# Reordering three stage borders of a hybrid mLSTM / gating / macaron block on one core

## The chip, the cores and the metric

The kernel runs on one core of a Trainium2 chip. The metric is the device time of one execution in microseconds (us). TensorE is called PE, VectorE DVE, ScalarE ACT, GpSimd POOL and SyncE SP; POOL and SP mostly start transfers here. PEld is the weight load of TensorE.

## The reference

One layer of a streaming encoder on x of 1024 tokens by 1024 features, in float32, with RMS norms ahead of every part:

```
x += 0.5 * SwiGLU_1(rmsnorm(x) * g1)            # d_ff = 2816
xn = rmsnorm(x) * gm;  P = xn @ w_mix_in
h_m = mlstm(P), 4 heads of 256;  h_s = spatial gating(P)
x += (sigmoid(g_m) * h_m + sigmoid(g_s) * h_s) @ w_mix_out
x += 0.5 * SwiGLU_2(rmsnorm(x) * g2)
out = rmsnorm(x) * final_g
```

## The kernel before

Tokens are held as two halves of 512 (h, or t, = 0 and 1); features lie on the 128 partitions, in eight tiles d = 0 to 7. A float32 operand is split into a rounded high part (ACT cast) and a remainder (DVE subtraction), and each product is three matmuls, high by high, high by low and low by high. One call of `prod` is 12 matmuls of 128x512.

Each SwiGLU input projection is done as a 2x2 block product with seven instead of eight block products. For that, `operands(i, get)` forms sums and differences of the two token halves (tiles "t1" to "t4" and "22"), for i = 0 to 3. While these do not exist yet, PE can only run products with half 0: "11" (features 0 to 3) and "21" (features 4 to 7) of a d_ff tile f. They are done ahead for the first `EARLY` = 9 tiles by `first_product(f)`: "11" into a PSUM bank, an ACT copy of the bank, "21" added into the same bank, an ACT Silu of it. Both results go to DRAM (`eb`) and come back when `group(f)` needs them. `group(f)` is the rest of a tile's work and needs all operands.

**FFN1's opening.** `scales(0)` sums the squares of the tokens (ACT for two token tiles, DVE `bn_stats` for two), forms 1/rms `r` and puts it on four diagonal matrices `dg`. `scaled(0, d)` then transposes and scales at once: a matmul of the token tile with `dg`. ACT and DVE split the result into xn, POOL rebuilds the sum and writes it to DRAM (`xs_`). Then come `first_product(0)`, `scales(1)` for half 1, and four rounds of two `first_product` calls, two `residual(d)` (plain transposes of both halves into `xd[2]`, the residual stream in DRAM) and `operands(i, get)`, where `get` takes half 0 from DRAM and half 1 from `scaled(1, d)` by way of ACT.

**FFN1 to mix.** `Stats` adds squares as the last down projection ends; `bcast` turns them into a scale tile: four small matmuls (L220), a chain of small DVE steps with one ACT square root, four DVE diagonals (L234), one matmul with ones (L237), an ACT copy (L239). `hook1` does this for half 1 at the very end of FFN1, although half 1's normed tiles are only made in the mix, after head 0.

**Mix to FFN2.** `mix_out(1, prev)` ends the mix with its output projection (L157 into `po`) and its own `bcast`; FFN2's first products come after it in the program.

Programs are handed to a scheduler that fixes each engine's order in advance: program order gives the priority, and an instruction that it expects to be ready may go ahead of an earlier one that it expects to wait. On the chip each engine then runs its list in that order. `t512` tiles come from a ring of four in FFN1 and FFN2; raw weights from a ring of three (`rawp`); operands of `operands` from a ring of six (`c512`); `bigp` holds 16 tiles for tokens, xn and operands.

Of the kernel before, what the change touches and what calls it, by code (L numbers as in the profile page):

```python
# [13 lines left out]
P = 128  # L14
S = 1024
D = 1024
NH = 512
# [1 line left out]
DFF = 2816  # L19
NF = DFF // P  # L20
BLOCKS = [(0, 3), (3, 3), (6, 3), (9, 3), (12, 3), (15, 3), (18, 4)]
EARLY = 9
SPAD = 40
MPAD = 24
HEADS = 4
# [8 lines left out]
def block_body(ctx, tc, x, ffn1_norm_g, ffn1_w_in, ffn1_w_out, mix_norm_g, w_mix_in, mlstm_conv_w,  # L34
# [228 lines left out]
    class Ffn:  # L263
# [35 lines left out]
            V.tensor_tensor(out=s, in0=a, in1=b, op=op)  # L299
            return s  # L300

        def first_product(self, f):
            r1, r2 = self.raw(f, 0, False), self.raw(f, 1, False)
            w1, w2 = self.unit(r1[:, :, 0, :]), self.unit(r2[:, :, 0, :])
            a = bank("mm")
            self.prod(a, w1, "11", True, False)
            e = self.hp.tile([P, 2, NH], F32, tag="h", name="early")
            A.copy(out=e[:, 0, :], in_=a)  # L308
            G.dma_start(out=self.eb[f][0], in_=e[:, 0, :])
            self.prod(a, w2, "21", False, True)  # L310
            A.activation(out=e[:, 1, :], in_=a, func=AF.Silu)
            G.dma_start(out=self.eb[f][1], in_=e[:, 1, :])

        def group(self, f):
            r1, r2 = self.raw(f, 0, True), self.raw(f, 1, True)
# [149 lines left out]
    def mix(mx, xnm):  # L465
# [122 lines left out]
        def sgu_v(xn):  # L588
            gz = [bigp.tile([P, D], F32, tag="big", name="gz") for _ in range(4)]
            stt = ss.tile([P, 4, 4, 6], F32, tag="stt", name="stt", bufs=1)  # L590
            gT = ss.tile([P, NC, 8], F32, tag="gT", name="gT")
            for c in range(4):
                if c == 0:
                    b = token_pair_wide(wmi, CZV, (CI, 8), xn)
                else:
                    b = token_pair(wmi, CZV + c * 2 * P, xn)
                for t in range(4):
                    if c == 0:
                        V.tensor_tensor(out=gT[:, t, :], in0=b[t][:, 2 * P:2 * P + 8], in1=bif, op=ALU.add)
                        src = b[t][:, 0:2 * P]  # L600
                    else:
                        src = b[t // 2][:, (t % 2) * 2 * P:(t % 2 + 1) * 2 * P]
                    dst = gz[t][:, c * 2 * P:(c + 1) * 2 * P]
                    A.activation(out=dst, in_=src, func=AF.Gelu)  # L604
                    V.bn_stats(out=stt[:, t, c, :], in_=dst)
                if c == 0:
                    gt = gates(gT)
            mv = ss.tile([P, 4, 2], F32, tag="mv", name="mv")
            for t in range(4):
                V.bn_aggr(out=mv[:, t, :], in_=stt[:, t].rearrange("p c s -> p (c s)"))  # L610
            r = rsqrt(mv[:, :, 1], 4, LN_EPS)
            for t in range(4):
                V.tensor_scalar(out=gz[t], in0=gz[t], scalar1=mv[:, t, 0:1], scalar2=r[:, t:t + 1], op0=ALU.subtract,
                                op1=ALU.mult)
            return gz, gt
# [159 lines left out]
        def mix_out(half, Ms):  # L775
            mh = []
            for ct in range(KT):
                mt = bigp.tile([P, 2, NH], F32R, tag="big", name="mh")
                split(Ms[ct], mt)
                mh.append(mt)  # L780
            st = Stats()
            for d in range(0, KT, 2):
                b = feature_pair(w_mix_out[0], d * P, mh, "po")
                for j in range(2):
                    xr = xrp.tile([P, NH], F32, tag="xr", name="xr")
                    nc.sync.dma_start(out=xr, in_=xd[0][half][d + j])
                    V.tensor_tensor(out=xr, in0=b[j], in1=xr, op=ALU.add)
                    nc.sync.dma_start(out=xd[1][half][d + j], in_=xr)
                    st.add(xr)
            return st.bcast()  # L790

        def reload(dram):
            def ld(d):
# [8 lines left out]
        for half in range(2):  # L802
            xn = xnm[half]
            if half == 0:
                setup()
                gz, gt = sgu_v(xn)
            cur = qkv(0, xn)
            if half == 1:
                bcs.append(mix_out(0, prev))
                gz, gt = sgu_v(xn)  # L810
            Ms = sgu_mix(gz)
            for h in range(HEADS):
                num = mlstm(h, half, *cur, gt)
                Gt = fillers(h, xn, Ms)
                merge(h, num, Gt, Ms)
                if h + 1 < HEADS:
                    cur = qkv(h + 1, xn)
                if h == 0:
                    if half == 0:
                        xnm[1] = normed(reload(xd[0][1]), "gm", xnm[1])  # L820
                    else:
                        xn2[0] = normed(reload(xd[1][0]), "g2", bcs[0], keep=xs_[1])
            prev = Ms
        bcs.append(mix_out(1, prev))
        return xn2[0], bcs

    with f1:
        ffn1 = Ffn(f1, "1", ffn1_w_in[0], ffn1_w_out[0])
        st2 = [Stats(), Stats()]
        dgs = []  # L830
        xns = []
        xnm = [None, None]

        def scales(h):
            dg = sp.tile([P, NH], F32, tag="bc", name="dg", bufs=2)
            ssq = sp.tile([P, 4, 2], F32, tag="ssq", name="ssq", bufs=2)
            stt = sp.tile([P, 2, 8, 6], F32, tag="sst", name="sst", bufs=1)
            for i in range(4):
                for t in range(2):
                    junk = t512()  # L840
                    A.activation(out=junk[:, 0:2 * P], in_=tok[h][i][:, t], func=AF.Square,
                                 accum_out=ssq[:, i:i + 1, t])
                    for j in range(2):
                        V.bn_stats(out=stt[:, t, 2 * i + j, :], in_=tok[h][i][:, t + 2, j, :])
# [14 lines left out]
            for t in range(4):  # L859
                V.tensor_scalar(out=dg[:, t * P:(t + 1) * P], in0=ident, scalar1=r[:, t:t + 1], scalar2=None,  # L860
                                op0=ALU.mult)
            dgs.append(dg)

        def scaled(h, d):
            ps = bank("mm")
            for t in range(4):
                PE.matmul(out=ps[:, t * P:(t + 1) * P], lhsT=tok[h][d % 4][:, t, d // 4, :],
                          rhs=dgs[h][:, t * P:(t + 1) * P], start=(t == 0), stop=(t == 3), skip_group_check=True)
            return ps

        def residual(d):
            xt = ffn1.hp.tile([P, 2, NH], F32, tag="h", name="xres")
            for h in range(2):
                ps = psm()
                for t in range(4):
                    PE.transpose(out=ps[:, t * P:(t + 1) * P], in_=tok[h][d % 4][:, t, d // 4, :], identity=ident)
                V.tensor_copy(out=xt[:, h, :], in_=ps)
                G.dma_start(out=xd[2][h][d], in_=xt[:, h, :])

        def get(j, i, t):  # L880
            b = ffn1.c512()
            if t == 0:
                G.dma_start(out=b, in_=xs_[0][4 * j + i])
            else:
                A.activation(out=b, in_=scaled(t, 4 * j + i), func=AF.Copy, scale=pc("g1", 4 * j + i))
            return b

        scales(0)
        for d in range(KT):
            ps = scaled(0, d)  # L890
            xt = bigp.tile([P, 2, NH], F32R, tag="big", name="xn")
            A.activation(out=xt[:, 0, :], in_=ps, func=AF.Copy, scale=pc("g1", d))
            V.scalar_tensor_tensor(out=xt[:, 1, :], in0=ps, scalar=pc("g1", d), in1=xt[:, 0, :].bitcast(F32),
                                   op0=ALU.mult, op1=ALU.subtract)
            xk = t512()
            G.tensor_tensor(out=xk, in0=xt[:, 0, :].bitcast(F32), in1=xt[:, 1, :].bitcast(F32), op=ALU.add)
            G.dma_start(out=xs_[0][d], in_=xk)
            xns.append(xt)
        ffn1.B["11"], ffn1.B["21"] = xns[:4], xns[4:]
        tok[1] = load_tokens(1)  # L900
        ffn1.first_product(0)
        scales(1)
        for i in range(4):
            ffn1.first_product(2 * i + 1)
            ffn1.first_product(2 * i + 2)
            for d in (i, i + 4):
                residual(d)
            ffn1.operands(i, get)

        def fin1(t, d, part, xt):  # L910
# [3 lines left out]
        def hook1(t, xs):  # L914
            if t == 0:
                xnm[0] = normed(xs, "gm", st2[0].bcast(), True)
            else:
                while todo:
                    spread()
                xnm[1] = st2[1].bcast()  # L920

        ffn1.run(xd[2], fin1, (1, 1), hook1)

    with ExitStack() as mx:
        open_psum(mx, 2, mm=3, po=2, ml=3)
        open_temps(mx, 2, 5)
        xn2, bcs = mix(mx, xnm)

    with ExitStack() as f2:
        open_psum(f2, 3, mm=6, ml=2)  # L930
# [11 lines left out]
            V.scalar_tensor_tensor(out=b, in0=b, scalar=pc("g2", d), in1=bcs[t], op0=ALU.mult, op1=ALU.mult)  # L942
            return b

        ffn2.first_product(0)
        for i in range(4):
            ffn2.first_product(2 * i + 1)
            ffn2.first_product(2 * i + 2)
            ffn2.operands(i, get2)

        PARTS = (1, 2)
# [59 lines left out]
```

## Time and profile before

| | us |
|---|---|
| median of 3 runs | 2328.27 |
| lowest, highest | 2324.36, 2329.82 |
| the profiled execution | 2329.39 |
| its span, first to last instruction | 2327.6 |
| PE busy in the span | 2278.7 |
| DVE, ACT, POOL busy | 1355.6, 992.7, 275.8 |

The profiled execution lies 1.1 us above the median, and 1.8 us of it lie outside the span. Busy time on PE is modelled from pipelined matmuls that overlap, so it overstates the work; spacing of matmuls tells more.

### The profile page before, as it was taken

What the parts mean: (1) busy time and instruction counts of PE and PEld (TensorE: products, weight loads), DVE (VectorE), ACT (ScalarE), POOL (GpSimd) and SP (SyncE); (2) the same over time, 40 slices, a digit from 0 to 9 for tenths busy, and PEclk for the clock granted to TensorE, in tenths of its full rate; (3) what the DMA queues carried; (4) which work ended last, traced back from release to release, by engine and by line L of the source; (5) the groups of instructions that cost most, each with busy time, mean ns of one, the idle gap of its engine ahead of it and who ended that gap; (6) DMA issues with size and microseconds to landing.
All of it is one profiled execution on the core that took longest, in us unless ns stands there. A gap on an engine that the chain in (4) does not pass through costs nothing. (4 is left out here: it accounts for less than half of the span.)

```text
span 2327.6 us, 29885 instructions
## 1 busy us (share of the span) xinstructions
PE 2278.7 (98%) x11295; PEld 1925.1 (83%) x11295; DVE 1355.6 (58%) x2401; ACT 992.7 (43%) x1586; POOL 275.8 (12%) x394
## 2 busy tenths in 40 slices
PE   6999999999999999999999999999899999999998
PEld 5788888888888988888889888888688888888887
DVE  5756545535567657556646575564775446346466
ACT  5433333333334445454434554543533333333432
POOL 3321220120111000000000000000212210210200
PEclk9999999999999999999999999999899999999999
DMA  6665763562544324322343253324747753744633
GB/s 217 227 135 129 149 122 74 106 129 59 114 154 132 105 73 127 98 84 82 96 150 100 83 161 92 91 81 128 225 139 157 143 120 72 132 90 87 122 100 109
DMA packets 277617, 278.95 MB, mean 120 GB/s; under 512 B 16473, under 2 KB 234201, under 8 KB 277473
## 3 DMA queue, kind: packets, MB, share of 16 engines
q1 hardware_dynamic: 235488, 180.49, 26.5%
q0 software_dynamic: 41728, 96.49, 21.0%
q8 instruction: 88, 1.44, 0.3%
q14 instruction: 57, 0.46, 0.1%
q10 hardware_dynamic: 256, 0.07, 0.0%
HBM read 196.22 MB, written 80.77 MB: 119 GB/s over the span
## 5 line engine op out<-in xcount | busy, mean ns | idle before, releaser
L293 PE MATMUL mm<-b,fw 128*128 128x512 f32 x2640 | 610.1, 390 | 2.0 <-ACT b L190 2.0
L293 PEld LDWEIGHTS mm<-b,fw 128*128 128x128 f32 x2640 | 496.5, 188 | 105.8 <-ACT b L190 2.4
L157 PE MATMUL mm<-xn,w 128*128 128x512 f32 x2304 | 545.8, 391 | 0.0
L157 PEld LDWEIGHTS mm<-xn,w 128*128 128x128 f32 x2304 | 426.8, 188 | 82.7
L390 PE MATMUL mm<-h,fw 128*128 128x512 f32 x1728 | 393.6, 389 | 0.0
L390 PEld LDWEIGHTS mm<-h,fw 128*128 128x128 f32 x1728 | 324.4, 188 | 67.3
L287 DVE TENSOR_TENSOR fw<-raw,fw 128x512 fp32r<-128x512 f32 (+1 forms) x228 | 144.1, 633 | 237.0 <-ACT fw L286 236.9
L293 PE MATMUL mm<-xn,fw 128*128 128x512 f32 x1056 | 257.6, 397 | 7.5 <-ACT early L308 7.5
L133 DVE TENSOR_TENSOR w<-raw,w 128x1024 fp32r<-128x1024 f32 (+2 forms) x146 | 176.5, 1209 | 142.8 <-ACT w L132 142.6
L383 POOL DMA_DIRECT2D xd<-c x192 | 165.9, 865 | 681.8 <-ACT c L382 670.6
L293 PEld LDWEIGHTS mm<-xn,fw 128*128 128x128 f32 x1056 | 199.6, 191 | 54.4 <-ACT early L308 12.0
L132 ACT CAST w<-raw 128x1024 fp32r<-128x1024 f32 (+2 forms) x146 | 151.3, 1038 | 153.9 <-PE mm L157 82.2
L382 ACT ACTIVATE c<-mm 128x512 f32<-128x512 f32 x192 | 114.7, 597 | 236.2 <-PE mm L390 172.7
L287 DVE TENSOR_TENSOR fw<-s,fw 128x512 fp32r<-128x512 f32 x176 | 121.3, 689 | 131.6 <-ACT fw L286 131.0
L286 ACT CAST fw<-raw 128x512 fp32r<-128x512 f32 (+1 forms) x228 | 130.3, 572 | 150.3 <-PE mm L293 86.3
L286 ACT CAST fw<-s 128x512 fp32r<-128x512 f32 x176 | 108.8, 618 | 133.8 <-PE mm L293 125.6
L171 PE MATMUL mm<-w,xn 128*128 128x256 f32 x1344 | 164.8, 283 | 0.6 <-ACT gz L604 0.5
L171 PEld LDWEIGHTS mm<-w,xn 128*128 128x128 f32 x1344 | 162.9, 192 | 1.7 <-ACT gz L604 0.7
L390 PE MATMUL mm<-h,wl 128*128 128x512 f32 (+1 forms) x480 | 95.6, 352 | 0.0
L190 ACT CAST h<-c 128x512 fp32r<-128x512 f32 x88 | 54.7, 622 | 89.4 <-DVE c L359 71.2
L157 PE MATMUL po<-mh,w 128*128 128x512 f32 x384 | 87.5, 389 | 0.0
L390 PEld LDWEIGHTS mm<-h,wl 128*128 128x128 f32 x480 | 77.7, 189 | 11.4 <-issue 0.5
(234 smaller groups left out, 2047.2 us busy)
## 6 DMA issues: line engine op xcount, KB each, us to landing
raw<-in_w_mix_in_dram SPq DMA_DIRECT2D x124, 512.0 KB, 3.8
raw<-in_ffn_w_in_dram SPq DMA_DIRECT2D x212, 256.0 KB, 4.7
xd<-c POOLq DMA_DIRECT2D x192, 256.0 KB, 5.4
raw<-in_ffn_w_out_dram SPq DMA_DIRECT2D x48, 384.0 KB, 3.1
eb<-early POOLq DMA_DIRECT2D x36, 256.0 KB, 3.4
c<-eb POOLq DMA_DIRECT2D x36, 256.0 KB, 3.2
xl<-xd POOLq DMA_DIRECT2D x32, 256.0 KB, 3.4
xr<-xd SPq DMA_DIRECT2D x32, 256.0 KB, 3.1
```

Of the source, the lines that this page charges most:

```text
L132: A.copy(out=w[:, 0, 0:n, :], in_=raw[:, 0:n, :])
L133: V.tensor_tensor(out=w[:, 1, 0:n, :], in0=raw[:, 0:n, :], in1=w[:, 0, 0:n, :].bitcast(F32), op=ALU.subtract)
L157: PE.matmul(out=banks[j], lhsT=w[:, a, i, j * P:(j + 1) * P], rhs=act[k][:, b, ts], start=(k == first and pi == 0), stop=(k == last and pi ...
L171: PE.matmul(out=o, lhsT=act[k][:, b, t * P:(t + 1) * P], rhs=w[:, a, i, :], start=(t % 2 == 0 and k == 0 and pi == 0), stop=(t % 2 == 1 an ...
L190: A.copy(out=dst[:, 0, :], in_=src)
L286: A.copy(out=w[:, 0], in_=src)
L287: V.tensor_tensor(out=w[:, 1], in0=src, in1=w[:, 0].bitcast(F32), op=ALU.subtract)
L293: PE.matmul(out=bank, lhsT=w[:, x, i, :], rhs=self.B[b][i][:, y, :], start=(start and i == 0 and pi == 0), stop=(stop and i == 3 and pi == 2),
L382: A.activation(out=xt, in_=o, func=AF.Copy, scale=0.5)
L383: G.dma_start(out=acc[t][d + j], in_=xt, accum_op=ALU.add)
L390: PE.matmul(out=o, lhsT=w[:, x, i, :], rhs=hs[i][:, y, ts], start=(i == 0 and pi == 0), stop=(i == n - 1 and pi == 2))
```

## The change

- FFN1, half 0: `turned(0, i)` transposes the token tiles plainly, as they arrive, within `scales(0)`; ACT copies one bank of a pair and DVE the other; the tiles go to the residual stream at once. `scales` now ends in a broadcast scale tile (a matmul with ones, as in `bcast`), and `normed` multiplies, splits and writes `xs_`.
- FFN1, half 1: `turned(1, i)` replaces `residual` and `scaled`; `get` forms the scaled tile on DVE in place of ACT.
- `first_products(fs)` does a pair of tiles: "11" of both, then "21" of both. `EARLY` is 10; `scales(1)` comes behind the first pair.
- FFN1 to mix: `hook1` leaves the statistics; their `bcast` is made in `sgu_v`, after `gates`.
- Mix to FFN2: `mix_out(1)` returns its statistics; the `bcast` comes behind FFN2's first pair.

```diff
-EARLY = 9
+EARLY = 10
+        def first_products(self, fs):
+            st = []
+            for f in fs:
+                w = self.unit(self.raw(f, 0, False)[:, :, 0, :])
+                a = bank("mm")
+                self.prod(a, w, "11", True, False)
+                e = self.hp.tile([P, 2, NH], F32, tag="h", name="early")
+                A.copy(out=e[:, 0, :], in_=a)
+                G.dma_start(out=self.eb[f][0], in_=e[:, 0, :])
+                st.append((f, a, e))
+            for f, a, e in st:
+                w = self.unit(self.raw(f, 1, False)[:, :, 0, :])
+                self.prod(a, w, "21", False, True)
+                A.activation(out=e[:, 1, :], in_=a, func=AF.Silu)
+                G.dma_start(out=self.eb[f][1], in_=e[:, 1, :])
...
                 if c == 0:
                     gt = gates(gT)
+                    if isinstance(xnm[1], Stats):
+                        xnm[1] = xnm[1].bcast()
...
-            return st.bcast()
+            return st
...
-        def scales(h):
-            dg = sp.tile([P, NH], F32, tag="bc", name="dg", bufs=2)
+        def scales(h, step=None):
+            dg = t512()
...
             for i in range(4):
+                if step is not None:
+                    step(i)
...
+            ps = psm()
+            PE.matmul(out=ps, lhsT=ones, rhs=dg, start=True, stop=True)
+            bc = sp.tile([P, NH], F32, tag="bc", name="bc", bufs=2)
+            A.copy(out=bc, in_=ps)
+            return bc
+
+        def turned(h, i):
+            xt = ffn1.hp.tile([P, 2, NH], F32, tag="h", name="xt")
+            for j in range(2):
+                ps = bank("mm")
                 for t in range(4):
+                    PE.transpose(out=ps[:, t * P:(t + 1) * P], in_=tok[h][i][:, t, j, :], identity=ident)
+                if j == 0:
+                    A.copy(out=xt[:, j, :], in_=ps)
+                else:
+                    V.tensor_copy(out=xt[:, j, :], in_=ps)
+                G.dma_start(out=xd[2][h][4 * j + i], in_=xt[:, j, :])
+            return xt
...
-                A.activation(out=b, in_=scaled(t, 4 * j + i), func=AF.Copy, scale=pc("g1", 4 * j + i))
+                V.scalar_tensor_tensor(out=b, in0=x2[:, j, :], scalar=pc("g1", d), in1=bc2, op0=ALU.mult, op1=ALU.mult)
...
+        xt = []
+        bc1 = scales(0, lambda i: xt.append(turned(0, i)))
+        xns = normed([xt[d % 4][:, d // 4, :] for d in range(KT)], "g1", bc1, keep=xs_[0])
         ffn1.B["11"], ffn1.B["21"] = xns[:4], xns[4:]
         tok[1] = load_tokens(1)
-        ffn1.first_product(0)
-        scales(1)
+        ffn1.first_products((0, 1))
+        bc2 = scales(1)
         for i in range(4):
-            ffn1.first_product(2 * i + 1)
-            ffn1.first_product(2 * i + 2)
-            for d in (i, i + 4):
-                residual(d)
+            ffn1.first_products((2 * i + 2, 2 * i + 3))
+            x2 = turned(1, i)
             ffn1.operands(i, get)
...
-                xnm[1] = st2[1].bcast()
+                xnm[1] = st2[1]
...
-        ffn2.first_product(0)
+        ffn2.first_products((0, 1))
+        bcs.append(st.bcast())
         for i in range(4):
-            ffn2.first_product(2 * i + 1)
-            ffn2.first_product(2 * i + 2)
+            ffn2.first_products((2 * i + 2, 2 * i + 3))
             ffn2.operands(i, get2)
```

## Rows read from the trace of the kernel before

**Rows 1.** The page's busy times: us, share of the span, instructions.

```profile
PE 2278.7 (98%) x11295; PEld 1925.1 (83%) x11295; DVE 1355.6 (58%) x2401; ACT 992.7 (43%) x1586; POOL 275.8 (12%) x394
```

**Rows 2.** Waits of PE: line, releaser: us in total, times, longest.

```profile
PE ml L106 <- DMA xtok<-in_x_dram: 11.6, 1, 11.6
PE mm L293 <- ACT early L308: 7.5, 5, 3.6
PE ml L237 <- DVE t L234: 6.2, 1, 6.2
```

**Rows 3.** Timeline of PE, the opening: start, us, instruction, count, idle before.

```profile
16.82 10.36 PE L867 MATMUL mm<-dg,xtok 128*128 128x128 f32 x64 [3.96 <-DVE dg L860]
26.94 11.01 PE L293 MATMUL mm<-xn,fw 128*128 128x512 f32 x47
41.55 5.73 PE L293 MATMUL mm<-xn,fw 128*128 128x512 f32 x13 [3.60 <-ACT early L308]
47.12 0.60 PE L876 MATMUL ml<-ident,xtok 128*128 128x128 f32 x4
47.56 1.95 PE L867 MATMUL mm<-dg,xtok 128*128 128x128 f32 x16
```

**Rows 4.** Timeline of ACT and DVE in the opening.

```profile
35.32 0.42 ACT L841 ACTIVATE t<-xtok 128x256 f32<-128x256 f32 x1 [4.26 <-POOL t L896]
...
45.05 0.87 DVE L860 TENSOR_SCALAR dg<-ident,r 128x128 f32<-128x128 f32 x4
...
47.08 0.60 ACT L311 ACTIVATE early<-mm 128x512 f32<-128x512 f32 x1 [1.73 <-PE mm L293]
```

**Rows 5.** Timeline of PE where FFN1's groups begin.

```profile
102.00 6.73 PE L293 MATMUL mm<-b,fw 128*128 128x512 f32 x28
110.70 39.09 PE L293 MATMUL mm<-b,fw 128*128 128x512 f32 x164 [1.96 <-ACT b L190]
```

**Rows 6.** Timeline of PE, FFN1 to mix.

```profile
720.60 1.02 PE L220 MATMUL ml<-ones,acc 128*128 128x1 f32 x8 [1.07 <-DVE acc L215]
...
725.45 1.39 PE L237 MATMUL ml<-t,ones 128*128 128x512 f32 x2
```

**Rows 7.** Timeline of PE, mix to FFN2.

```profile
1629.66 2.20 PE L157 MATMUL po<-mh,w 128*128 128x512 f32 x9
1634.54 1.84 PE L220 MATMUL ml<-ones,acc 128*128 128x1 f32 x8 [2.68 <-DVE acc L215]
1642.56 2.05 PE L237 MATMUL ml<-t,ones 128*128 128x512 f32 x2 [6.18 <-DVE t L234]
1643.62 17.29 PE L293 MATMUL mm<-xn,fw 128*128 128x512 f32 x64
...
1697.27 3.11 PE L293 MATMUL mm<-b,fw 128*128 128x512 f32 x13
```

**Rows 8.** Timeline of DVE and ACT, mix to FFN2: weights of the first products.

```profile
1632.51 1.28 DVE L287 TENSOR_TENSOR fw<-raw,fw 128x512 fp32r<-128x512 f32 x2
...
1640.09 0.62 ACT L286 CAST fw<-raw 128x512 fp32r<-128x512 f32 x1 [3.27 <-DMA raw<-in_ffn_w_in_dram]
```

**Rows 9.** Chain of waits, in order of time: a stretch of FFN2's first products.

```profile
1661.13 78.92 PE mm L293 x344
```

**Rows 10.** Groups of DVE instructions by form, 1645 to 1690: busy, mean ns.

```profile
L191 DVE TENSOR_TENSOR b<-c,b 128x512 fp32r<-128x512 f32 x20 | 13.5, 685 | 0.1
L942 DVE SCALAR_TENSOR_TENSOR c<-c,par,bc 128x512 f32<-128x512 f32 x8 | 5.8, 748 | 2.8 <-ACT bc L239 2.8
```

**Rows 11.** Windows: stretch, length, busy of PE, PEld, DVE, ACT, POOL, granted clock, DMA share, GB/s.

```profile
12.00:17.00 5.00, 1.04 (x6) 0.64 (x5) 4.45 (x20) 2.33 (x7) 0.00 (x0) 1.00 0.51 150
18.00:20.00 2.00, 2.00 (x12) 2.00 (x11) 0.66 (x2) 0.69 (x1) 0.00 (x0) 1.00 0.48 136
42.00:44.00 2.00, 2.00 (x6) 1.52 (x6) 1.05 (x4) 1.97 (x4) 0.33 (x1) 0.50 0.39 133
1654.00:1690.00 36.00, 35.77 (x155) 28.30 (x155) 28.98 (x47) 23.47 (x43) 13.03 (x24) 1.00 0.91 286
```

More of the change, by code (lines that the diff above doesn't have):

```diff
@@ L300, in combine @@
             return s
[L302 to L312, printed above, removed]
+        def first_products(self, fs):
[13 more added lines that the diff above has]
+                G.dma_start(out=self.eb[f][1], in_=e[:, 1, :])
         def group(self, f):
@@ L808, in mix @@
             if half == 1:
-                bcs.append(mix_out(0, prev))
+                bcs.append(mix_out(0, prev).bcast())
                 gz, gt = sgu_v(xn)
@@ L823, in mix @@
             prev = Ms
-        bcs.append(mix_out(1, prev))
-        return xn2[0], bcs
+        return xn2[0], bcs, mix_out(1, prev)
     with f1:
@@ L829, in block_body @@
         st2 = [Stats(), Stats()]
-        dgs = []
-        xns = []
         xnm = [None, None]
-        def scales(h):
-            dg = sp.tile([P, NH], F32, tag="bc", name="dg", bufs=2)
+        def scales(h, step=None):
+            dg = t512()
             ssq = sp.tile([P, 4, 2], F32, tag="ssq", name="ssq", bufs=2)
@@ L861, in scales @@
                                 op0=ALU.mult)
[L862 to L874, printed above, removed]
-                for t in range(4):
-                    PE.transpose(out=ps[:, t * P:(t + 1) * P], in_=tok[h][d % 4][:, t, d // 4, :], identity=ident)
-                V.tensor_copy(out=xt[:, h, :], in_=ps)
-                G.dma_start(out=xd[2][h][d], in_=xt[:, h, :])
+            ps = psm()
@@ L880, in get @@
         def get(j, i, t):
             b = ffn1.c512()
+            d = 4 * j + i
             if t == 0:
-                G.dma_start(out=b, in_=xs_[0][4 * j + i])
+                G.dma_start(out=b, in_=xs_[0][d])
             else:
-                A.activation(out=b, in_=scaled(t, 4 * j + i), func=AF.Copy, scale=pc("g1", 4 * j + i))
+                V.scalar_tensor_tensor(out=b, in0=x2[:, j, :], scalar=pc("g1", d), in1=bc2, op0=ALU.mult, op1=ALU.mult)
             return b
-        scales(0)
@@ L889, in block_body @@
[L889 to L898, printed above, removed]
+        xt = []
@@ L926, in block_body @@
         open_temps(mx, 2, 5)
-        xn2, bcs = mix(mx, xnm)
+        xn2, bcs, st = mix(mx, xnm)
     with ExitStack() as f2:
```

## Prediction

> **What bounds the kernel now.** I read the page's busy times first: PE is busy 98% of the span and the next engine, DVE, 58% as long [rows 1]. So time can be won only where PE stands still, runs at the low clock, or does work that could be left out. The waits of PE name such places: 11.6 us at the start for the first transpose, 7.5 us in five waits on the ACT copy of an early product, 6.2 us at one matmul with ones, L237 [rows 2]. Then I followed PE in time through the three borders that the diff touches.
>
> The opening: PE does the scaled transposes of half 0 from 16.82 to 27.2, products only from 26.94, 47 of them, stands 3.60 us until 41.55, and does the next 13 in 5.73 us, 0.44 us each, at a granted clock of 0.50, the lower level of 1.2 GHz [rows 3, 11]. At the full clock a product of 128x512 takes 78.92 / 344 = 0.229 us in such a stretch [rows 9]. The Silu of tile 1 starts at 47.08, so 48 products are done there [rows 4]. The groups begin at 102.00; after 28 of their matmuls PE waits 1.96 us for the last operand and goes on at 110.70, with 9 x 24 + 28 = 244 products behind it [rows 5].
>
> FFN1 to mix: PE waits 1.07 us for the end of the sum of squares at L220 and stops for a matmul with ones, 1.39 us [rows 6].
>
> Mix to FFN2: the output projection ends at 1629.66 + 2.20 = 1631.86, and the first FFN2 product starts at 1643.62. In these 11.8 us PE does 3.9 us of statistics and waits 2.68 + 6.18 us, although two weight tiles of the first products are split by 1632.51 + 1.28 = 1633.8, the first by 1633.2 [rows 7, 8]. At 1697.27 the nine tiles and four group matmuls, 220 products, are behind it.
>
> **The change part by part, FFN1's opening.** It goes through the time at which 48 products are done.
>
> Statistics. The diagonals reach PE at 16.82 now [rows 3]. The new copies come between them: four on ACT (0.60 each, the nearest row being the Silu of a bank) and four on DVE (I use 0.69, the mean of a 128x512 split) [rows 4, 10], 2.4 and 2.8 us, side by side. PE cannot help before 11.6, since its first transpose in order is that of the parameters, and then has eight banks of four transposes, 0.60 each or 4.8 us, so they end at 16.4 or later [rows 2, 3]. In before ACT and DVE have read the tokens by then; in after, statistics of the last token tiles stand behind copies that wait for PE. Bounds: 0 if the copies lie behind the statistics, 5.2 if both engines' copies are paid in turn; I take 4.5, near the upper one, since the program puts the transposes of a tile ahead of its squares. Diagonals at PE: 21.3.
>
> Broadcast and first split: matmul with ones 1.39 (row of the mix border; 2.05 at the low clock), ACT copy 0.60, so the scale is there at 23.3; then 0.75 for the product with it and 0.6 for the cast: first product at 24.7 against 26.94. From there DVE sets the pace: eight tiles of 0.748 + 0.685 us are 11.5 us, and two weight splits of 1.4 us lie between [rows 10]. The last tile is ready at 36.2, the last six products take 1.4: 48 products at 37.6, 9.5 us ahead of 47.08. The pair is what fills PE here: six matmuls of 0.229 per feature tile, 1.4 us, against 1.43 us of DVE. POOL issues eight more transfers, of the residual tiles, ahead of the `xs_` writes; in 12 to 17 it is idle and the DMA share is 0.51 [rows 11], so I charge nothing; without that room they would delay the tokens of half 1, which are needed only after the first pair.
>
> To the same point with 244 products: 196 x 0.229 = 44.9; eight banks of transposes of half 1, 4.8; one broadcast, 1.0 (half the 2.05 of the low clock). Gone are the scaled transposes of half 1, 16 matmuls in 1.95 us per round [rows 3], and half 0's share of the plain ones. For stalls I take 6: 7.5 - 3.6 = 3.9 on ACT copies, 1.96 on the last operand [rows 2, 5]. Pairs put 12 other products behind each "11", 2.7 us against a copy of 0.6, so the bound below is 2; above it is 11, if the squares of half 1 again stop ACT as at 35.32, where they waited 4.26 us for a `t512` tile [rows 4]. Sum 37.6 + 44.9 + 4.8 + 1.0 + 6 = 94.3, against 110.70: **16.4 us less**.
>
> Can DVE keep up? A round costs it four weight splits, five operand splits, four sums (0.69 each, 9.0), two scaled tiles (1.5) and a copy (0.7): 11.1 us. PE has 48 x 0.229 + 2 x 0.60 = 12.2. DVE stays below PE, with a margin of 1.1 per round. FFN2's rounds are the nearest sample: they move the same twelve 256 KB tiles per round, at a DMA share of 0.91, and PE runs on [rows 9, 11]. So I charge nothing for the tenth early tile either: its 24 products move, and its two results go through DRAM.
>
> **FFN1 to mix.** The wait of 1.07 us goes; L220 and L237 move behind `gates`, same cost, and nothing needs the scale until head 0 is through. But the last normed tile of half 0 comes from the same DVE list, so PE may wait there anyway: 0 to 2.5, I take **1.0**. An extra table load on ACT is covered, as ACT is idle more than half of the time [rows 1].
>
> **Mix to FFN2.** Products start at 1633.2. The bcast brings no transfers; the four raw loads of the pair are now first on SP. Three fit in the ring before the border. The fourth's cast is at 1640.09 [rows 8] and its split done at 1641.4; three products of 12 last until 1633.2 + 8.2 = 1641.4. Then 220 x 0.229 = 50.4, the statistics at the full clock (half of 1.84 + 2.05) about 2, stalls 2 (0 to 6): 1687.6 against 1697.27, **9.6 us less**. Of this 2.7 are the 13 products that start at the low clock now. Behind the waiting L237 on PE stand the next pair's products. The scale may come at 1650 rather than 1645; DVE then needs its four rounds of about 10 us, to 1690, just about when the ten tiles are through (1633.2 + 55 + 4 = 1692).
>
> Sum: 16.4 + 1.0 + 9.6 = 27.0, from 2329.39: 2302.4 for an execution like the profiled one, which lies 1.1 above the median; against the median 2301.3. I say 2302.
>
> **A rule weighed.** In 12 to 17 PE does little but transposes, and the column reads 1.00 there and in 18 to 20 [rows 11]; so the sum lets the first products run at the full clock. The Trainium skill, "TensorE: Matmul & The Clock Gate", Part 4 (PE-mode transpose), says that transposes do not bring the full clock as matmuls do. By it the change swaps the work that warms PE ahead of its first products for work that does not, and the sum would be 2.7 us longer; the trace leans that way in one point, 12 scaled matmuls in 2 us at 18 to 20 [rows 11] against 16 in 1.95 us later [rows 3].
>
> **Rivals.**
> - The opening stays late. ACT's squares wait for the transposes, then for `t512` tiles held by the `xs_` writes, the early copies queue behind them, PE stands and falls to the low clock. For it: this chain exists now (4.26, then 3.60, then 13 x 0.21 = 2.7). Against: POOL's sum is gone. Price 10 us: 2312.
> - First products at the low clock after plain transposes, a mechanism by itself: 13 x (0.44 - 0.229) = 2.7: 2305. The rule above is this case.
> - The opening is hidden: the copies lie behind the statistics (-4.5): 2297.
> - FFN2's start runs out of raw weights, or its operands end late: 7 of the 9.6 are lost: 2309.
> - The change does not do what it says: the scheduler already fills gaps with later work, and orders the queues much as before: 2326.
> - Slower: operands become the last thing. `get` needs the half 1 scale, whose matmul L237-like sits in PE's fixed order; if it comes late, rounds of 11.1 us on DVE follow one after another, and the groups start four rounds, 44.4 us, later. At a scale at 48 (diagonals at 45.05 to 45.92 now [rows 4]) they end at 92 and cost nothing. At 66 the FFN1 gain is gone; from 77 on the kernel is slower; at 85, 2310 + 19 + some 6 of low clock = 2335. For it: DVE takes over work from ACT. Against: the scale has 37 us to spare over where it is now.
>
> **Numbers.** Chances: forecast 0.50 (its own range 2296 to 2309), opening late 0.17, low clock 0.10, opening hidden 0.07, FFN2 0.06, no change 0.04, slower 0.06. A difference below 0.2% (4.7 us) is about what a measurement of this kernel cannot tell from none. Faster: the first five, 0.90, less 0.02 for an opening late enough to lose all. Same 0.05, slower 0.07. Range: below, hidden statistics (4.5) and stalls at their bound of 2 (4): 2293. Above, late opening with FFN2's loss halved: 2317. Left out are no change, slower, and tails, under 0.2.
>
> **What the profile after would show.** L867 and POOL's sums gone; about 48 early products done near 38 us; FFN1's groups running freely by 95 instead of 110.7; no idle of PE over 2 us between the output projection and FFN2's first product, clock 1.00 there; L237's wait of 6.2 gone. Wrong, if the first product comes after 28, if waits on ACT early copies stay near 7 us, if DVE's operands end after 100, or if PE waits at 1640 for raw weights.

## The result, and the profile after

The changed kernel took 2302.09 us in the median of four runs (2297.41 to 2302.86), the kernel before 2328.49 (2324.36 to 2329.82). The ratio is 0.9885, with a 95% interval of 0.9867 to 0.9903: the medians differ by 26.4 us, and by the ratio the change is 1.15% faster. The forecast was 2302.0. The profiled execution has a span of 2300.0 us against 2327.6. The page's busy times (us, share of the span, instructions) answer to [rows 1]:

```profile
PE 2263.1 (98%) x11171; PEld 1908.0 (83%) x11171; DVE 1355.5 (59%) x2409; ACT 992.9 (43%) x1589; POOL 270.1 (12%) x394
```

PE has 124 matmuls less and is busy 15.6 us less; the other 12 us of the span's 27.6 are idle time of PE that is gone. Where it went is read stage by stage. I took five marks in both timelines of PE (us):

| mark | before | after | after is ahead by |
|---|---|---|---|
| FFN1's last down projections begin (`mm<-h,wl`) | 671.87 | 653.37 | 18.5 |
| first product of the mix (`mm<-w,xn`) | 717.43 | 698.92 | 18.5 |
| first gating product (`ml<-wsT,gz`) | 807.01 | 789.19 | 17.8 |
| half 1's output projection begins (`po<-mh,w`) | 1588.06 | 1570.98 | 17.1 |
| FFN2's last down projections begin | 2262.12 | 2234.74 | 27.4 |
| end of the span | 2327.6 | 2300.0 | 27.6 |

By stage: the opening gave 18.5 us (forecast 16.4), FFN1 to mix gave -0.7 (forecast 1.0), the rest of the mix -0.7 (nothing was forecast), mix to FFN2 10.3 (forecast 9.6). The total of 27.6 is near the 27.0 of the sum, with errors of up to 3 us of both signs in it.

The waits of PE in after (line, releaser: us in total, times, longest) answer to [rows 2]:

```profile
PE ml L106 <- DMA xtok<-in_x_dram: 6.7, 1, 6.7
PE mm L878 <- DMA xtok<-in_x_dram: 3.9, 1, 3.9
PE ml L868 <- DVE t L865: 3.6, 1, 3.6
...
PE mm L293 <- ACT xn L190: 2.1, 1, 2.1
PE mm L293 <- ACT early L309: 1.9, 2, 1.3
PE mm L293 <- ACT b L190: 1.6, 1, 1.6
PE ml L495 <- DMA t<-in_sgu_w_s_dram: 1.4, 1, 1.4
```

The 7.5 us on early copies are 1.9, and the 6.2 at L237 are gone. New are 3.6 and 2.1 before and behind the opening's broadcast (L868), where before had 3.96 in front of its scaled transposes [rows 3], and 1.4 at L495, which the forecast did not have.

The timeline of PE in the opening, which answers to [rows 3] and [rows 5] (start, us, instruction, count, idle before):

```profile
11.90 0.45 PE L106 MATMUL ml<-ident,t 128*128 128x128 f32 x1 [6.68 <-DMA xtok<-in_x_dram]
12.14 5.69 PE L878 MATMUL mm<-ident,xtok 128*128 128x128 f32 x27
21.41 2.08 PE L868 MATMUL ml<-t,ones 128*128 128x512 f32 x2 [3.58 <-DVE t L865]
25.60 25.00 PE L293 MATMUL mm<-xn,fw 128*128 128x512 f32 x94 [2.11 <-ACT xn L190]
...
89.88 4.81 PE L293 MATMUL mm<-b,fw 128*128 128x512 f32 x20
96.28 40.45 PE L293 MATMUL mm<-b,fw 128*128 128x512 f32 x172 [1.59 <-ACT b L190]
```

The broadcast starts at 21.41 (forecast 21.3), the first product at 25.60 (24.7). At 96.28 there are 240 + 20 = 260 products behind PE, 16 more than the 244 at which the forecast counted. Counted back by 16 x 0.229, this answers to 244 products at 92.6, against 94.3 forecast and 110.70 before.

The second Silu on ACT, where 48 products are done in after, and what DVE waits for ahead of it:

```profile
40.22 0.60 ACT L315 ACTIVATE early<-mm 128x512 f32<-128x512 f32 x1 [0.99 <-PE mm L293]
```

```profile
30.28 0.75 DVE L248 SCALAR_TENSOR_TENSOR t<-xt,par,bc 128x512 f32<-128x512 f32 x1 [1.59 <-DMA xs<-t]
31.57 0.75 DVE L248 SCALAR_TENSOR_TENSOR t<-xt,par,bc 128x512 f32<-128x512 f32 x1 [0.54 <-DMA xs<-t]
```

And the windows of the same stretch (length, busy of PE, PEld, DVE, ACT, POOL, granted clock, DMA share, GB/s):

```profile
20.00:22.00 2.00, 0.58 (x1) 0.50 (x2) 1.81 (x7) 0.31 (x1) 0.00 (x0) 0.71 0.92 305
22.00:26.00 4.00, 1.89 (x3) 0.40 (x2) 1.85 (x3) 1.61 (x3) 0.68 (x2) 0.50 1.06 300
26.00:30.00 4.00, 3.95 (x9) 2.58 (x9) 2.69 (x5) 1.45 (x3) 1.48 (x3) 0.50 1.15 339
30.00:34.00 4.00, 3.99 (x15) 2.93 (x14) 3.19 (x5) 1.50 (x3) 1.08 (x2) 0.87 1.11 370
```

48 products were done at 40.2, not 37.6. Two things lie on top of each other: the granted clock falls while PE waits for the broadcast and still reads 0.50 (1.2 GHz) in 26 to 30, nine products in 4 us; and DVE waits for a `t512` tile that an `xs_` write still holds, with the DMA share above 1.0. Both had been put at nothing. The same Silu in before, at 47.08 [rows 4], is no mark of 48 products: PE had 47 + 13 = 60 behind it [rows 3]. The 48th began at 41.55 there, behind the wait of 3.60, and was done near 42.0; so after is 1.8 us ahead at 48 products.

Mix to FFN2, timeline of PE (answers to [rows 7]):

```profile
1570.98 43.81 PE L157 MATMUL po<-mh,w 128*128 128x512 f32 x192
1614.62 0.84 PE L293 MATMUL mm<-xn,fw 128*128 128x512 f32 x3
1616.17 7.79 PE L293 MATMUL mm<-xn,fw 128*128 128x512 f32 x33 [0.70 <-DVE fw L287]
1624.56 3.04 PE L293 MATMUL mm<-xn,fw 128*128 128x512 f32 x12 [0.60 <-ACT early L309]
1627.44 0.95 PE L220 MATMUL ml<-ones,acc 128*128 128x1 f32 x8
1628.24 4.79 PE L293 MATMUL mm<-xn,fw 128*128 128x512 f32 x20
1632.87 1.05 PE L237 MATMUL ml<-t,ones 128*128 128x512 f32 x2
1633.36 39.81 PE L293 MATMUL mm<-xn,fw 128*128 128x512 f32 x172
```

The first product follows the projection at once. L220 and L237 stand between products with no wait, at 0.95 and 1.05 where they took 1.84 and 2.05. PE waits 1.3 us in all here.

### The profile page after: what moved, and what is told of

Its sections match the earlier page's. It is cut to its first block, busy times and chain, and to the rows that moved or that the text cites. A ratio compares the mean times of both kernels' runs of the same rounds, so it can differ in the third digit from the quotient of the medians.

```text
span 2300.0 us, 29669 instructions
## 1 busy us (share of the span) xinstructions
PE 2263.1 (98%) x11171; PEld 1908.0 (83%) x11171; DVE 1355.5 (59%) x2409; ACT 992.9 (43%) x1589; POOL 270.1 (12%) x394
## 3 DMA queue, kind: packets, MB, share of 16 engines
q0 software_dynamic: 42368, 98.59, 21.4%
```

## The experiments

Each is the changed kernel with one edit, if not said otherwise. Beside medians and ratios to before I compare stages by three stretches of the timeline: the mark of FFN1's last projections (opening; 653.37 in after), from there to the first gating product (FFN1 to mix; 135.82), and from the end of half 1's output projection to FFN2's last projections (mix to FFN2; 619.95, before 630.25).

**The FFN2 border undone** (`scale_in_mix`).

```diff
-        return xn2[0], bcs, mix_out(1, prev)
+        bcs.append(mix_out(1, prev).bcast())
+        return xn2[0], bcs
...
         ffn2.first_products((0, 1))
-        bcs.append(st.bcast())
```

> The changed kernel with the mix-to-FFN2 border undone alone: the scale chain of mix_out(1) is back in the mix, ahead of FFN2's first products, still in pairs. Theory (this border is worth what the two traces' marks say, 28.7 - 17.1 = 11.6 us): about 2312 to 2314, PE standing some 9 us between the output projection and FFN2's first product, clock 0.50 there. Rival (the border itself hides little; the gain there came from the pairs and the tenth early tile): 2302 to 2305.

Measured: 2309.15, ratio 0.9914 [0.9901, 0.9928]; mix to FFN2 629.02, 9.1 us longer than in after. The old wait is back, in the timeline of PE:

```profile
1624.43 2.05 PE L237 MATMUL ml<-t,ones 128*128 128x512 f32 x2 [6.26 <-DVE t L234]
1625.49 57.03 PE L293 MATMUL mm<-xn,fw 128*128 128x512 f32 x240
```

So 9.1 of this border's 10.3 us hang on the chain's place. The time lies between the two ranges that had been expected.

**That border alone, on the kernel before** (`ffn2_border_only`): nine tiles, one by one, and the chain behind the first.

```diff
-        bcs.append(mix_out(1, prev))
-        return xn2[0], bcs
+        return xn2[0], bcs, mix_out(1, prev)
...
         ffn2.first_product(0)
+        bcs.append(st.bcast())
```

> The kernel before with the mix-to-FFN2 border alone: the scale chain of mix_out(1) behind FFN2's first product, singles and nine early tiles as before. Theory (the border alone carries the FFN2 gain): 2317 to 2319, 9 to 11.6 us under the kernel before. Rival (it needs the pair in front of the chain, since one tile covers only 5.4 us): 2321 to 2324.

Measured: 2321.21, ratio 0.9968 [0.9955, 0.998]; mix to FFN2 623.8, 6.4 us less than before. One tile's products cover less: L237 still waits 2.16 us for the diagonals. Moving alone gives 6.4, pairs and tenth tile alone 1.2 (630.25 - 629.02), both together 10.3: the pair is cover for the chain. The time falls into the rival's range, not the theory's. No run takes the tenth early tile away by itself.

**One tile at a time** (`singles`).

```diff
-        ffn1.first_products((0, 1))
+        ffn1.first_products((0,))
+        ffn1.first_products((1,))
...
-            ffn1.first_products((2 * i + 2, 2 * i + 3))
+            ffn1.first_products((2 * i + 2,))
+            ffn1.first_products((2 * i + 3,))
```
and the same for `ffn2`.

> The changed kernel with first products one tile at a time in the program, all else kept. Theory (the scheduler fills a bank's copy with the next tile's products anyway, so pairs are worth little): 2302 to 2304, waits of PE on early copies at most 4 us. Rival (pairs are what removed the waits on early copies, 7.5 us to 1.9): 2306 to 2312.

Measured: 2308.74, ratio 0.9915 [0.9902, 0.9929]; opening 4.2 us later, mix to FFN2 4.1 longer. PE waits 6.9 us in six waits for early copies (1.9 in after), the longest:

```profile
92.53 4.61 PE L293 MATMUL mm<-xn,fw 128*128 128x512 f32 x12 [3.86 <-ACT early L309]
```

A tile's "21" waits for the ACT copy of its "11" bank, ACT has other work ahead of that copy, and PE does nothing past a waiting matmul. The theory that other tiles' work would fill this gap anyway is refuted.

**Half 1 by scaled matmuls again** (`scaled_half1`): `scales(1)` returns the diagonals, `get` multiplies on PE and copies on ACT.

```diff
-                V.scalar_tensor_tensor(out=b, in0=x2[:, j, :], scalar=pc("g1", d), in1=bc2, op0=ALU.mult, op1=ALU.mult)
+                ps = bank("mm")
+                for q in range(4):
+                    PE.matmul(out=ps[:, q * P:(q + 1) * P], lhsT=tok[1][i][:, q, j, :], rhs=bc2[:, q * P:(q + 1) * P],
+                              start=(q == 0), stop=(q == 3), skip_group_check=True)
+                A.activation(out=b, in_=ps, func=AF.Copy, scale=pc("g1", d))
```

> The changed kernel with half 1 scaled within its transposes again: 16 scaled matmuls (1.95 us) per round on PE for get and an ACT copy in place of the DVE product; its plain transposes for the residual stream stay. Theory (PE bounds the rounds): 4 x 1.95 = 7.8 us more, less 1.1 for the broadcast, so 2308 to 2310. Rival (DVE bounds the rounds, which loses 1.5 us of work per round): 2298 to 2303.

Measured: 2310.9, ratio 0.9928 [0.9916, 0.9941]; opening 7.6 us later. 16 matmuls in 1.95 us per round are 7.8 us of PE time back, and the waits on early copies are 5.0.

**Half 0 opened as before** (`scaled_half0`): diagonals, scaled matmuls, POOL's sums; its plain transposes in the rounds.

```diff
-        bc1 = scales(0, lambda i: xt.append(turned(0, i)))
-        xns = normed([xt[d % 4][:, d // 4, :] for d in range(KT)], "g1", bc1, keep=xs_[0])
+        dg0 = scales(0)
+        for d in range(KT):
...
+                PE.matmul(out=ps[:, t * P:(t + 1) * P], lhsT=tok[0][d % 4][:, t, d // 4, :],
+                          rhs=dg0[:, t * P:(t + 1) * P], start=(t == 0), stop=(t == 3), skip_group_check=True)
...
+            G.tensor_tensor(out=xk, in0=xt[:, 0, :].bitcast(F32), in1=xt[:, 1, :].bitcast(F32), op=ALU.add)
...
+            turned(0, i)
             x2 = turned(1, i)
```

> The changed kernel with half 0 opened as before the change (scaled matmuls, POOL sums, plain transposes of half 0 for the residual stream inside the rounds), all else kept. Theory (of the 18.5 us of the opening, half 1's scaled matmuls made 7.6 and half 0 the rest): FFN1's last stage 10 to 11 us later than in the changed kernel, 2311 to 2314. Rival (DVE's operands, which end the opening, stay where they are): 3 to 6 us, 2305 to 2308.

Measured: 2308.74, ratio 0.9912 [0.9899, 0.9926]; opening 6.8 us later, below what the theory expected and above what its rival did. 48 products were done at 41.66, only 1.4 later than in after; the rest comes in the rounds, where the transposes of half 0 stand again (16 in 1.91 us instead of 8 in 1.04, four times 0.9), and from a wait of 3.23 on the last operand (1.59 in after). So with pairs the old way of half 0 is hardly slower to its 48 products; what it costs is mostly the work it leaves for later.

**The scale of the mix back in the hook** (`scale_in_hook`).

```diff
-                    if isinstance(xnm[1], Stats):
-                        xnm[1] = xnm[1].bcast()
...
-                xnm[1] = st2[1]
+                xnm[1] = st2[1].bcast()
```

> The changed kernel with the FFN1-to-mix border undone alone: half 1's scale chain is back at the end of FFN1. Theory (the move earns nothing: between the first wide product and the first gating product the lead fell from 18.5 to 17.8 us): 2300 to 2303, the same. Rival (the forecast: 1.0 us won by the move, up to 2.5): 2303 to 2305.

Measured: 2299.73, ratio 0.9872 [0.9857, 0.9887], no slower than the change; FFN1 to mix 133.33, 2.5 us less than in after and 1.8 less than before. The timelines of PE give both differences. After, with the two windows in which its slow stretch lies:

```profile
702.51 3.80 PE L184 MATMUL mm<-w,xn 128*128 128x264 f32 x29 [0.34 <-DVE xn L191]
707.72 0.66 PE L495 MATMUL ml<-ident,t 128*128 128x128 f32 x4 [1.41 <-DMA t<-in_sgu_w_s_dram]
...
725.92 1.05 PE L220 MATMUL ml<-ones,acc 128*128 128x1 f32 x8
726.84 6.29 PE L171 MATMUL mm<-w,xn 128*128 128x256 f32 x38
```

```profile
726.00:728.00 2.00, 2.00 (x15) 2.00 (x16) 0.92 (x6) 1.33 (x3) 0.00 (x0) 0.85 0.24 84
728.00:730.00 2.00, 2.00 (x12) 2.00 (x11) 1.83 (x9) 1.10 (x2) 0.00 (x0) 0.50 0.00 0
```

With the scale in the hook:

```profile
701.07 1.02 PE L220 MATMUL ml<-ones,acc 128*128 128x1 f32 x8 [0.82 <-DVE acc L215]
701.95 2.93 PE L184 MATMUL mm<-w,xn 128*128 128x264 f32 x22
704.72 1.02 PE L237 MATMUL ml<-t,ones 128*128 128x512 f32 x2
```

And `scaled_half1`, which has the scale behind `gates` as after has it:

```profile
733.23 4.79 PE L171 MATMUL mm<-w,xn 128*128 128x256 f32 x38
```

The wait of 0.82 at L220 is exchanged for 0.34 + 1.41: PE now reaches the transposes of `sgu_w_s` (L495) before that load, which the moved chain used to cover. That is 0.9 of the 2.5. The other 1.5 is the clock: behind the 4x4 transposes, a wait of 0.63 and the eight small matmuls of L220 it falls to the lower level, and the same 38 products take 6.29 us there against 4.79 in `scaled_half1`, where the clock stayed at 1.00 and the stage took 133.44 (PE waited 1.2 us once at its start, and not at L495). In seven of the eight traces with the scale behind `gates` a window at 0.50 to 0.53 follows this L220; in the three with the scale in the changed kernel's hook none does. Before had a low stretch of its own: 0.86 in 717 to 725, and 22 products of L184 in 4.16 us against 2.93 in the hook version:

```profile
721.49 4.16 PE L184 MATMUL mm<-w,xn 128*128 128x264 f32 x22
```

**The parameter transpose later** (`params_later`): L106 is issued behind the turns, so that the transposes need not wait for it.

```diff
-    pt = psm()
-    PE.transpose(out=pt[:, 0:P], in_=rows, identity=ident)
-    V.tensor_copy(out=par, in_=pt[:, 0:P])
...
         bc1 = scales(0, lambda i: xt.append(turned(0, i)))
+        pt = psm()
+        PE.transpose(out=pt[:, 0:P], in_=rows, identity=ident)
+        V.tensor_copy(out=par, in_=pt[:, 0:P])
```

> The changed kernel with the parameter transpose behind the token transposes in the program. Theory (the parameters' late transfers hold PE until 11.9 and so the copies ahead of the statistics): transposes follow the tokens from 3.9 us, diagonals some 3 us earlier, at 18 to 19 instead of 21.4, 2298 to 2300. Rival (the last token tiles, at 11.8, and the copies set the statistics in any case): 2301 to 2303.

Measured: 2301.03, ratio 0.9878 [0.9864, 0.9891]; opening 653.17, as in after. The transposes ran from 3.80, but PE then waited 6.77 us and the broadcast began at 21.74. So the expected gain did not come, but part of its mechanism did. The scale `r` of half 0 was finished 1.8 us sooner, by the instruction that starts at 18.38 against 20.21 in after. DVE then had a weight split in its list ahead of the diagonals, and that split waited for a cast on ACT, which waited 2.71 us for raw weights:

```profile
18.38 0.16 DVE L195 TENSOR_TENSOR r<-r,nw 128x4 f32<-128x4 f32 x1
19.55 0.62 ACT L283 CAST fw<-raw 128x512 fp32r<-128x512 f32 x1 [2.71 <-DMA raw<-in_ffn_w_in_dram]
20.20 0.69 DVE L284 TENSOR_TENSOR fw<-raw,fw 128x512 fp32r<-128x512 f32 x1 [1.66 <-ACT fw L283]
20.81 0.87 DVE L862 TENSOR_SCALAR t<-ident,r 128x128 f32<-128x128 f32 x4
```

In after the diagonals (20.49) stand ahead of that split (21.28). What the edit is worth with the diagonals ahead of the split is open.

**Tiles of its own for `normed`** (`own_tiles`): half 0's scaled tiles come from `ffn1.tx`, not from the `t512` ring.

```diff
-            t = t512()
+            t = mk() if mk else t512()
...
+                     mk=lambda: ffn1.tx.tile([P, 2, NH], F32, tag="tx", name="xk")[:, 0, :])
```

> The changed kernel with half 0's normed tiles in tiles of their own (idle operand tiles) instead of the ring of four t512, so that no write of xs has to land before the next product with the scale. Theory (the ring and the transfers, not DVE, pace the first 48 products: DVE waited 1.85 + 1.59 + 0.54 us for them): 48 products done by 37.5 instead of 40.2, 2299 to 2301. Rival (the low clock paces them): 48 products at 39.5 or later, 2302.

Measured: 2299.81, ratio 0.9879 [0.9864, 0.9894]; opening 652.64. The waits for `xs_` writes are gone, and yet 48 products are done at 40.17, as in after: PE, at 0.50 until about 31, is the slower of the two. The time came as the theory said, but not for its reason.

**Two more matmuls behind the transposes** (`warm`).

```diff
+            if h == 0:
+                wb = psm()
+                for q in range(2):
+                    PE.matmul(out=wb, lhsT=ones, rhs=xt[3][:, 0, :], start=(q == 0), stop=(q == 2 - 1))
             ps = psm()
             PE.matmul(out=ps, lhsT=ones, rhs=dg, start=True, stop=True)
```

> The changed kernel with two extra matmuls of 128x512 with ones (float32, result unused) between the last transposes of half 0 and the broadcast. Theory (transposes leave PE at the low level): each takes 2.05 us, and the first products are no sooner; 2301 to 2303. Rival (the opening is at the full level until PE has stood for some time): each takes 1.0 us, the broadcast 1.0 instead of 2.08, and the first 13 products run at 0.23 instead of 0.45 us each, 2299 to 2301.

Measured: 2299.82, ratio 0.9875 [0.9861, 0.989]; opening 650.58, 2.8 us sooner. That is little beyond what executions differ by: `scale_in_mix`, with the opening of after, reached the mark at 651.17. PE in the timeline:

```profile
17.85 1.98 PE L870 MATMUL ml<-xt,ones 128*128 128x512 f32 x4
21.46 1.12 PE L872 MATMUL ml<-t,ones 128*128 128x512 f32 x2 [1.63 <-DVE t L865]
24.70 25.37 PE L293 MATMUL mm<-xn,fw 128*128 128x512 f32 x94 [2.11 <-ACT xn L190]
```

Right behind 27 transposes the extra matmuls run at 0.50 us for each record of 128x512, half of the 1.04 at L868 in after, and so does the broadcast. The transposes had not left PE at the lower level; it fell while PE waited. Behind the broadcast PE waits again, and 26 to 30 reads 0.50 here too, so the rival's first products at 0.23 did not come.

The clock column is no evidence of the level ahead of the first product. Two windows of the kernel before:

```profile
8.00:11.00 3.00, 0.00 (x0) 0.00 (x0) 1.46 (x6) 1.93 (x10) 0.00 (x0) 1.00 0.82 224
24.00:26.00 2.00, 2.00 (x20) 2.00 (x19) 1.49 (x2) 1.59 (x3) 1.67 (x3) 1.00 0.99 290
```

It reads 1.00 in 8 to 11, where PE has not run one instruction, and it reads 1.00 both in 18 to 20, with 12 scaled matmuls [rows 11], and in 24 to 26, with 20 of the same. The pace tells the level, and `params_later` has transposes at both levels, on either side of a fall that the column does show (PE's timeline, and a window):

```profile
11.94 0.66 PE L875 MATMUL mm<-ident,xtok 128*128 128x128 f32 x4 [2.51 <-ACT xt L877]
13.86 1.10 PE L875 MATMUL mm<-ident,xtok 128*128 128x128 f32 x4 [1.27 <-DVE xt L879]
14.00:15.00 1.00, 0.96 (x4) 0.56 (x4) 1.00 (x4) 1.00 (x4) 0.89 (x2) 0.50 0.13 49
```

By this pace the opening's transposes in after, 27 in 5.69 us or 0.21 each, start at the lower level, and in the rounds 8 take 1.03 us, 0.13 each. Since the extra matmuls right behind the transposes run at the upper level, PE rose to it while it did nothing but transposes.

**Both limits removed** (`filled`): tiles of its own, the scale in the hook, and extra matmuls on both sides of the broadcast (three ahead, two behind).

```diff
...
+                for q in range(3):
+                    PE.matmul(out=wb, lhsT=ones, rhs=xt[3][:, 0, :], start=(q == 0), stop=(q == 3 - 1))
...
             PE.matmul(out=ps, lhsT=ones, rhs=dg, start=True, stop=True)
...
+                for q in range(2):
+                    PE.matmul(out=wb, lhsT=ones, rhs=dg, start=(q == 0), stop=(q == 2 - 1))
...
```

> The changed kernel with the FFN1-to-mix border undone, half 0's normed tiles in tiles of their own, and five extra matmuls with ones (results unused) that keep PE busy between half 0's transposes and the first products: three before the broadcast, two behind it. Theory (two limits lie over one another in the opening, the low clock and the ring of four tiles; each alone changed nothing, both together do): granted clock 1.00 from 20 to 32 us, first products 0.23 us each, 48 done by 37.5 to 38.5 instead of 40.2; with the 2.5 us of the border, 2296 to 2299. Rival (a third limit, the raw weights or ACT): 48 products still at 39.5 or later, 2299 to 2301.

Its partner, the same without the extra matmuls (`hook_own`):

> The same without the extra matmuls. Theory: 48 products at 40.2, paced by the low clock, 2298 to 2300. Rival (own tiles are worth something by themselves): below the kernel with the extra matmuls or level with it.

Measured: `filled` 2298.98, ratio 0.9868 [0.9854, 0.9881]; `hook_own` 2297.52, 0.9868 [0.9855, 0.9882]. In the traces `filled` opens 6 us sooner (647.23; `hook_own` 653.20), with 48 products done at 36.01 (40.86). Its windows:

```profile
22.00:26.00 4.00, 3.06 (x10) 1.43 (x9) 3.85 (x7) 1.97 (x4) 1.63 (x3) 1.00 1.10 307
26.00:30.00 4.00, 4.00 (x19) 3.07 (x17) 4.00 (x8) 2.29 (x4) 1.63 (x3) 1.00 1.09 371
```

19 products in 26 to 30 where after had nine. So the low clock is shown as a cause of the late 48 products: the two kernels differ in the extra matmuls alone. The part of the ring is not shown by itself. At the low clock it changes nothing (`own_tiles`), and no run has the ring of four with PE at the upper level throughout. Over whole runs, however, the two kernels cannot be told apart: the profiled run of `hook_own` has a span of 2300.5, its other three 2294.7 to 2295.6, those of `filled` 2294.8 to 2297.1. No trace shows at which clock the other runs of `hook_own` opened. Of the versions run, these two have the lowest ratio, but their intervals overlap that of the change.

## Why the prediction was right, point by point

- **The opening: right in the sum, two terms mis-sized, of opposite sign.** Diagonals at PE 21.4 (21.3 forecast), first product 25.6 (24.7), 48 products at 40.2 (37.6): 2.6 late. The steps that failed are "the sum lets the first products run at the full clock" and, by a share that no run separates, "I charge nothing" for POOL's extra transfers. `filled` takes both away and reaches 36.0. They were paid for by the stalls: of the 6 us allowed up to the groups, 1.29 + 1.59 came, near the lower bound of 2, since pairs cover the copies (`singles`: 4.2 us of this opening). At 244 products that is 92.6 instead of 94.3. That the forecast met the median within 0.1 us is in part luck: errors of 2.6 and 3.1 us cancel here, and the 2.1 us that the opening gave beyond its forecast stand against 1.7 and 0.7 that FFN1 to mix and the rest of the mix fell short.
- **Where the opening's gain lies: misread.** The prediction put 9.5 of its 16.4 us ahead of the 48th product, since it took 47.08 for the time of that product in before. There 60 products were done at 47.08; the 48th was done near 42.0 (41.55 + 0.44, [rows 3]). At 48 products after is 1.8 us ahead, at the groups 110.70 - 92.6 = 18.1, so 16.3 us are won behind the first pair, in the rounds. The sum was not touched, as it adds up the changed kernel's own terms, but the reason that it gives for most of the gain, earlier first products, is wrong.
- **What the opening's 18.5 us consist of.** Undone one at a time, half 1's scaled matmuls cost 7.6, half 0's way 6.8, the pairs 4.2: 18.6 in all. Behind the 48th product, which these three had done at 40.34, 41.66 and 41.21, they cost 7.5, 5.3 and 3.2 of it. The parts share waits, and each stands on one trace, so that sum is a check on the size and no proof of three independent terms.
- **The rival "first products at low clock".** Its event came, at about its price: 2.6 late at 48 products, by clock and ring together. Its reason was wrong. The rule of the Trainium skill, "TensorE: Matmul & The Clock Gate", Part 4 (PE-mode transpose), that transposes do not bring the full clock, does not show here: by `warm` matmuls run at 2.4 GHz directly behind them, and the wait of 3.58 for the diagonals is what precedes the fall. The prediction's own evidence did not bear on it: the column's 1.00 in 12 to 17 and 18 to 20 is no reading (`warm`), and its 12 slower matmuls at 18 to 20 were scaled matmuls and not transposes. The forecast had taken PE's wait into the start time and not into the clock.
- **FFN1 to mix: wrong in sign, small in size.** "The wait of 1.07 us goes" held. "0 to 2.5" missed that a matmul chain taken out from ahead of a load uncovers the load (1.41 at L495), and that its small matmuls in a new place can let the clock fall (1.5). [rows 6] held a hint, L237 at 1.39 us: in the hook version it takes 1.02, and the low stretch in before was there to be seen.
- **Mix to FFN2: right.** 10.3 against 9.6; `scale_in_mix` gives 9.1 of it to the chain's place. PE did not wait for raw weights, and the scale at 1632.87 delayed nothing. The forecast let the first product start at 1633.2, 1.3 us behind the projection, when its weights were split; it came at once, on the cast of the weights, and PE waited 0.70 us for the split behind it.
- **DVE.** It kept up: one wait of 1.59 on the last operand. The rival that operands end last had no part.

## What to carry to other kernels

A dependent chain at a stage's border holds up an engine that runs its list in order, and it is hidden by issuing it behind enough of the next stage's work: here that was worth 6.4 us behind one tile and 9.1 behind a pair. Before moving it, list what it covered in its old place (a load, the clock), since that becomes the next wait. When a wait on TensorE is costed, cost the clock of the work behind it too, from the granted-clock column of the nearest wait in the trace before, and check the column by the pace of like instructions. Count the products behind a mark before two kernels are compared there: the same Silu stood behind 60 products in one and 48 in the other.

## What the runs showed of the hardware that was not expected

- Small matmuls among busy work can be followed by a fall of the clock: behind the 4x4 transposes and eight 128x1 matmuls it read 0.50 for some 3 us (0.85, 0.50 and 0.80 in three windows of 2 us from 726 on) although PE counted as busy for the whole 726 to 734. Why it did not fall in `scaled_half1` is open.
- PE reached the upper level of the clock while it did nothing but transposes, and transposes are slower at the lower level: four took 1.10 us at 0.50 and 0.66 at 1.00 (`params_later`).
- The clock column can read 1.00 where it says nothing of PE: in before it does so in 8 to 11, ahead of PE's first instruction, and at 12 as at 20 scaled matmuls in 2 us.
- The same opening ran differently in different executions: in `scale_in_mix`, which does not touch it, the 27 transposes took 4.48 us where after has 5.69, the column reads 1.00 in 20 to 22 where after has 0.71, the broadcast took 1.13 us against 2.08, and the first product came at 23.83.
